# Weight sums of a Strassen-form projection taken from DRAM instead of formed by GpSimd

## The chip, the cores and the metric

The kernel runs on one core of a Trainium2 chip. The metric is the device time of one execution in microseconds (us). The engines are named TensorE (PE in the profile; PEld are its weight loads), VectorE (DVE), ScalarE (ACT), GpSimd (POOL) and SyncE (SP, which here only issues transfers).

## The reference

Two layers, each with two sub-layers on x of 512 tokens by 1024 features, all in float32:

```
for i in range(DEPTH):                                     # DEPTH = 2
    mix = mixer_sublayer(x, w_in[i], ...)                  # pooling mixer + bidirectional scan
    x = layer_norm(ALPHA * x + mix, ln1_g[i], ln1_b[i])
    ffn = conv_ffn(x, w_up[i], ffn_conv_w[i], ffn_conv_b[i], w_down[i])
    x = layer_norm(ALPHA * x + ffn, ln2_g[i], ln2_b[i])

def conv_ffn(x, w_up, ffn_conv_w, ffn_conv_b, w_down):
    h = dwconv_centred(x @ w_up, ffn_conv_w, ffn_conv_b)
    gate, val = jnp.split(h, 2, axis=-1)
    return (jax.nn.gelu(gate, approximate=False) * val) @ w_down
```

The scan of the mixer works on 32 heads, taken here in 8 units of 4 heads. w_down is 2816 by 1024. The change concerns the last product, with w_down, and the place in the mixer where the new transfers are issued.

## The kernel before, in words

Every float32 product is made of three TensorE passes on values split in a high part (wh, ah) and a remainder (wl, al). A weight block is loaded into a tile wraw (two places), ScalarE copies its rounded high part into wh (L90) and VectorE subtracts to get wl (L91); three places each for wh and wl. This is class WeightStream: a list of loads, and an order of cuts (`get`, `fill`) that runs ahead of TensorE. All loads go through SP's queue in the order of the list; a load waits there until its place is free.

A layer runs through the mixer, in which the eight units each make a decay matrix per head (m, fetched by ScalarE's queue as `m<-acd`, masked by GpSimd in L994, exponentiated by ScalarE in L1001), a state (xw by GpSimd in L1051, stp on TensorE, s in L1076) and an output y, begun by GpSimd in L1057 as `y = xtok * d_skip`; then through the up projection (TensorE into fg), and then the down stage (TensorE into dp_v, dp_x, dp_y, dp_z and a few more).

The down stage is in Strassen form (`strassen_projection`). The 22 k-tiles of w_down stand in 11 pairs, and each pair has four blocks of 128 by 512: b00, b01 (upper k-tile, left and right half) and b10, b11 (lower k-tile). Seven products take the place of eight, at the price of sums of blocks: t1 and t3 (L137, L138), t2 (L126) and t4 (L154) are formed by GpSimd in the kernel before, from blocks that lie in wraw. t1 and t3 replace their inputs in wraw; t2 goes into scratch (xths, xtls), and t4 replaces t2 there. The sums of the activations are made in the up stage; four of the seven are kept in SBUF, three (384 KB a pair) are spilled to DRAM (`asp<-r`, L1368) and fetched again in the down stage (`xtls<-asp`, L619, two places) and cut into dp_h and dp_l (L624, L625) one pair behind the fetch.

The loop over the first nine pairs, with the cuts `d` (b00 and b11) and `s` (t1 and t3), reads:

```
for i in range(n - 2):
    d, s = ws.get(), ws.get()
    both(vb, (tags[i], 3), d, 1, f, False)
    both(xb, ...); both(yb, ...); both(zb, ...)
    fetch(i)
    if i:
        cut(i - 1)
```

`both` makes two products of three passes each, so a pair takes 24 matmuls of 512 columns here and 18 in the lower phase (t2, b10, t4). A layer's down stage has 7 x 11 x 2 x 3 = 462.

TensorE's order is written out by hand. The orders of the other engines come from a scheduler, which places each instruction by priority and by when its inputs are ready.

Of the kernel before, what the change touches and what calls it, by code (L numbers as in the profile page):

```python
# [9 lines left out]
F32 = mybir.dt.float32  # L10
# [12 lines left out]
NL = 2  # L23
# [15 lines left out]
class WeightStream:  # L39
# [3 lines left out]
    def __init__(self, nc, tc, pool, plan, ahead, raw_bufs, bufs):  # L43
        self.nc, self.tc, self.pool = nc, tc, pool
        self.plan = plan
        self.subs = [(i, j) for i, r in enumerate(plan) for j in r["order"]]
        self.ahead = ahead
        self.raw_bufs, self.bufs = raw_bufs, bufs
        self.raw = {}
        self.done = {}  # L50
        self.next_raw = 0
        self.next_sub = 0
        self.pos = 0
        self.seq = []
        self.extra = {}
# [21 lines left out]
    def _split(self, s):  # L77
        i, view = self.seq[s]
        self.load(i + 1)
        src = view(self.raw[i])  # L80
        _, a, b = src.shape
        if s in self.extra:
            pool, bufs = self.extra[s]
        else:
            pool, bufs = self.pool, self.bufs
        h = pool.tile([P, 1024], F32R, tag="wh", name=f"wh{s}", bufs=bufs)
        l = pool.tile([P, 1024], F32R, tag="wl", name=f"wl{s}", bufs=bufs)
# [19 lines left out]
class StrassenWeights:  # L107
# [4 lines left out]
    def __init__(self, nc, tc, pairs):  # L112
        self.nc, self.tc, self.pairs = nc, tc, pairs
        self.t2 = {}
        self.raw0 = None

    def open(self, tiles):

        for t in tiles:
            for i in range(t.shape[1]):  # L120
                self.t2[len(self.t2)] = (t, i)
        self.make_t2(0, self.raw0)

    def make_t2(self, i, raw):
        t, j = self.t2[i]
        self.nc.gpsimd.tensor_tensor(  # L126
            t[:, j, :], raw[:, 1024:1536], raw[:, 512:1024], op=ALU.subtract
        )

    def direct(self, raw):  # L130

        return raw.rearrange("p (a b) -> p a b", a=2)[:, :, 0:512]

    def sums(self, i, raw):

        g = self.nc.gpsimd
        g.tensor_tensor(raw[:, 1536:2048], raw[:, 1024:1536], raw[:, 512:1024], op=ALU.subtract)  # L137
        g.tensor_tensor(raw[:, 512:1024], raw[:, 512:1024], raw[:, 0:512], op=ALU.subtract)  # L138
        if i:
            self.make_t2(i, raw)  # L140
        else:
            self.raw0 = raw
        return raw.rearrange("p (a b) -> p a b", a=2)[:, :, 512:1024]

    def two(self, q):
        t, j = self.t2[2 * q]
        return t[:, j : j + min(2, self.pairs - 2 * q), :]

    def lower(self, q, o, raw):

        t = self.two(q)
        n = t.shape[1]
        b = raw[:, o : o + n * 512].rearrange("p (a b) -> p a b", a=n)
        self.nc.gpsimd.tensor_tensor(t, b, t, op=ALU.subtract)  # L154
        return b

    def plan(self, w, first):

        raws, direct, sums = [], [], []
        for i in range(self.pairs):  # L160
            a, b = 2 * i * P, (2 * i + 1) * P
            raws.append({"srcs": [w[a : a + P, :].unsqueeze(1),
                                  w[b : b + P, 512:1024].unsqueeze(1)], "order": range(2)})
            direct.append((first + i, self.direct))
            sums.append((first + i, partial(self.sums, i)))
        seq = []
        for i in range(self.pairs - 2):
            seq += [direct[i], sums[i]]
        seq += direct[-2:] + sums[-2:]
        odd = w.rearrange("(k two p) c -> two p k c", two=2, p=P)[1, :, :, 0:512]  # L170
        lower, t2, t4 = [], [], []
        for i in range(0, self.pairs, 4):
            n = min(4, self.pairs - i)
            r = first + len(raws)
            raws.append({"srcs": [odd[:, i : i + n, :]], "order": range(n)})
            for k in range(0, n, 2):
                q = (i + k) // 2
                lower.append((r, partial(self.lower, q, k * 512)))
                t2.append((r if q else r - 1, lambda raw, q=q: self.two(q)))
                t4.append((r, lambda raw, q=q: self.two(q)))  # L180
# [44 lines left out]
def weight_plan(l, w_in, pool_w, w_ssd_proj, w_out, w_up, w_down, down):  # L225
# [71 lines left out]
    r, s = down.plan(w_down[l], len(raws))  # L297
# [4 lines left out]
def tile_hybrid_pool_ssd_convffn_encoder(  # L302
# [60 lines left out]
    downs = [StrassenWeights(nc, tc, KF // 2) for _ in range(NL)]  # L363
# [134 lines left out]
    class Norm:  # L498
# [28 lines left out]
        def add(self, c, c0, ps, first=False, last=False):  # L527
# [76 lines left out]
    def strassen_projection(l, name, sw, tags, pool, spill, norm):  # L604
# [7 lines left out]
        sw.open([scratch[0], scratch[1][:, : n - KD, :]])  # L612
        again = scratch[1][:, 3:6, :].rearrange("p a b -> p (a b)").rearrange(
            "p (s a b) -> p s a b", s=2, a=3)

        second = {}

        def fetch(i):
            nc.sync.dma_start(again[:, i % 2], spill[i])  # L619

        def cut(i):
            h = pool.tile([P, 4, 256], F32R, tag=f"ah{i}", name=f"{name}h{i}")
            lo = pool.tile([P, 4, 256], F32R, tag=f"al{i}", name=f"{name}l{i}")
            nc.scalar.copy(h[:, :3], again[:, i % 2])  # L624
            nc.vector.tensor_tensor(lo[:, :3], again[:, i % 2], h[:, :3], op=ALU.subtract)  # L625
# [20 lines left out]
        for i in range(n - 2):  # L646
# [12 lines left out]
            if i:  # L659
                cut(i - 1)  # L660
# [12 lines left out]
        for i in (n - 2, n - 1):  # L673
# [3 lines left out]
            cut(i - 1)  # L677
# [3 lines left out]
        for cc in range(2):  # L681
            norm.add(2 + cc, 512, zb[cc])
# [7 lines left out]
        for q in range(nq - 2):  # L690
# [5 lines left out]
            if q == 0:  # L696
                cut(n - 1)
# [70 lines left out]
    for l in range(NL):  # L768
# [264 lines left out]
        def unit_job(u, xtok, zs, xjobs):  # L1033
# [23 lines left out]
            nc.gpsimd.tensor_tensor(  # L1057
# [3 lines left out]
            )  # L1061
            ytiles[u] = (xtok, y)
# [278 lines left out]
        for j in range(KF):  # L1341
# [83 lines left out]
```

## Time and profile before

| | us |
|---|---|
| median of 3 runs | 1990.12 (1989.95 to 1991.82) |
| the profiled execution | 1992.83 |
| its span on the core | 1991.0 |
| TensorE busy | 1931.9 (97%) |
| VectorE busy | 1348.4 (68%) |
| ScalarE busy | 998.4 (50%) |
| GpSimd busy | 609.0 (31%) |

Layer 0's down stage runs from 872 to 993 us, layer 1's from 1857 to 1979. Matmuls overlap in the records: the distance from one start to the next is the time that one costs, not the length that its row gives.

### The profile page before, as it was taken

Reading aid. Unit: us, or ns where it says so; the run is one execution under the profiler, and the core shown is the slowest. Engines: PE = TensorE matmul, PEld = TensorE weight load, DVE = VectorE, ACT = ScalarE, POOL = GpSimd, SP = SyncE. Lnnn points to the kernel's source line nnn. Section 1 sums busy time; section 2 is a strip of 40 time slices with the busy share of each in tenths; the row PEclk is TensorE's granted clock in tenths of the full one; section 3 lists DMA queues with packets and bytes.
Section 4 is the critical chain, followed back from the end, with each engine's and each line's share of the span. In section 5 each row is a group of like instructions: output and inputs, shape, how many; then the busy total and the mean of one; then the engine's idle time right before and its main releaser. Section 6 shows DMA issues by size and latency. Waiting matters only on the chain.

```text
span 1991.0 us, 27368 instructions
## 1 busy us (share of the span) xinstructions
PE 1931.9 (97%) x10449; PEld 1616.0 (81%) x10449; DVE 1348.4 (68%) x1945; ACT 998.4 (50%) x1665; POOL 609.0 (31%) x578
## 2 busy tenths in 40 slices
PE   8999999999999999998999999999999999999997
PEld 7878798988888888876788878989888888888765
DVE  5668576775556656679985685667656566666898
ACT  4767666644333444444457776656443334444443
POOL 1244424241111111168303343242411111111773
PEclk9999999999999999999999999999999999999999
DMA  5444434233241334345225344343332414333541
GB/s 159 123 119 117 127 93 140 86 113 115 76 164 49 121 112 134 106 153 190 83 90 160 106 112 124 110 124 105 85 111 92 168 43 130 121 101 116 180 154 51
DMA packets 174691, 232.19 MB, mean 117 GB/s; under 512 B 7872, under 2 KB 128868, under 8 KB 174560
## 3 DMA queue, kind: packets, MB, share of 16 engines
q1 hardware_dynamic: 152144, 178.80, 28.3%
q10 hardware_dynamic: 17712, 34.08, 7.0%
q0 software_dynamic: 4704, 17.56, 2.5%
q8 instruction: 83, 1.36, 0.3%
q14 instruction: 48, 0.39, 0.1%
HBM read 217.31 MB, written 13.11 MB: 116 GB/s over the span
## 4 chain that ended last, share of the span: by engine, by line
PE 78%; DVE 6%; issue 6%; POOL 4%; DMA 3%; ACT 3%; SPq 0%; POOLq 0%; ACTq 0%; DVEq 0%
PE fg L382 7%; PE fg L381 7%; PE fg L383 7%; PE spp L381 3%; PE zp L381 3%; PE spp L382 3%; PE spp L383 3%; PE zp L382 3%; PE zp L383 3%; PE xp L381 3%; DVE wl L91 3%; PE xp L383 3%; PE xp L382 3%; PE stp L1068 2%; PE ydp L1019 2%
## 5 line engine op out<-in xcount | busy, mean ns | idle before, releaser
L91 DVE TENSOR_TENSOR wl<-wraw,wh 128x1024 fp32r<-128x1024 f32 (+1 forms) x330 | 454.1, 1377 | 251.6 <-ACT wh L90 250.0
L90 ACT CAST wh<-wraw 128x1024 fp32r<-128x1024 f32 (+1 forms) x330 | 341.2, 1035 | 503.6 <-PE fg L382 158.0
L383 PE MATMUL fg<-xthm,wl 128*128 128x512 f32 x640 | 249.0, 389 | 0.0
L381 PE MATMUL fg<-xthm,wh 128*128 128x512 f32 x640 | 249.0, 389 | 0.0
L382 PE MATMUL fg<-xtlm,wh 128*128 128x512 f32 x640 | 249.0, 389 | 0.0
L1001 ACT ACTIVATE m<-m,nac 128x128 f32<-128x128 f32 x512 | 159.6, 392 | 52.2 <-POOL m L994 51.7
L994 POOL TENSOR_SCALAR_AFFINE_SELECT m<-m 128x512 f32<-128x512 f32 x128 | 95.0, 765 | 183.5 <-DMA m<-acd 162.9
L381 PEld LDWEIGHTS fg<-xthm,wh 128*128 128x128 f32 x640 | 120.1, 188 | 25.0
L383 PEld LDWEIGHTS fg<-xthm,wl 128*128 128x128 f32 x640 | 120.1, 188 | 24.9
L382 PEld LDWEIGHTS fg<-xtlm,wh 128*128 128x128 f32 x640 | 120.1, 188 | 24.9
L1109 POOL TENSOR_TENSOR y<-y,yo 128x256 f32<-128x256 f32 x96 | 85.4, 898 | 101.6 <-DVE yo L1101 98.8
L381 PE MATMUL spp<-yth,wh 128*128 128x512 f32 x256 | 110.3, 431 | 0.5 <-ACT yth L1149 0.5
L382 PE MATMUL spp<-ytl,wh 128*128 128x512 f32 x256 | 101.2, 395 | 0.7 <-DVE ytl L1150 0.7
L383 PE MATMUL spp<-yth,wl 128*128 128x512 f32 x256 | 101.1, 395 | 0.0
L479 DVE SCALAR_TENSOR_TENSOR xc<-xp,pcwc,xc 128x510 f32<-128x510 f32 (+1 forms) x128 | 95.2, 745 | 7.2 <-ACT xc L473 5.7
L1002 DVE TENSOR_TENSOR m<-m 128x512 f32<-128x512 f32 x64 | 46.7, 730 | 64.8 <-ACT m L1001 55.5
L1051 POOL TENSOR_TENSOR xw<-xtok,wst 128x768 f32<-128x768 f32 x32 | 51.3, 1621 | 121.9 <-ACT xtok L943 99.0
L1363 POOL TENSOR_TENSOR r<-cvv,cg 128x512 f32<-128x512 f32 x22 | 28.4, 1292 | 175.1 <-issue 130.4
L381 PE MATMUL zp<-wh,xthf 128*128 128x256 f32 x256 | 77.6, 303 | 0.0
L1286 POOL TENSOR_TENSOR g<-g,acc 128x512 f32<-128x512 f32 x16 | 27.5, 1720 | 162.3 <-ACT g L1247 150.3
L381 PE MATMUL zp<-wh,xthi 128*128 128x256 f32 x256 | 77.1, 301 | 0.0
L382 PE MATMUL zp<-wl,xthf 128*128 128x256 f32 x256 | 73.0, 285 | 0.0
(403 smaller groups left out, 5214.0 us busy)
## 6 DMA issues: line engine op xcount, KB each, us to landing
wraw<-in_w_in_dram SPq DMA_DIRECT2D x56, 1024.0 KB, 5.5
wraw<-in_w_up_dram SPq DMA_DIRECT2D x44, 1024.0 KB, 5.2
m<-acd ACTq DMA_DIRECT2D x64, 512.0 KB, 4.9
wraw<-in_w_ssd_proj_dram SPq DMA_DIRECT2D x16, 1024.0 KB, 5.1
wraw<-in_w_down_dram SPq DMA_DIRECT2D x22, 512.0 KB, 3.6
asp<-r POOLq DMA_DIRECT2D x22, 384.0 KB, 2.9
xtls<-asp SPq DMA_DIRECT2D x22, 384.0 KB, 3.8
wraw<-in_w_in_dram SPq DMA_DIRECT2D x16, 512.0 KB, 5.3
```

Source lines behind the costliest of these rows:

```text
L90: self.nc.scalar.copy(hv, src)
L91: self.nc.vector.tensor_tensor(lv, src, hv, op=ALU.subtract)
L381: mm(lhsT=ah, rhs=bh, start=first, stop=False)
L382: mm(lhsT=ah, rhs=bl, start=False, stop=False)
L383: mm(lhsT=al, rhs=bh, start=False, stop=last)
L479: nc.vector.scalar_tensor_tensor(dst[:, o0:o1], ps[:, o0 + s : o1 + s], tap, dst[:, o0:o1], op0=ALU.mult, op1=ALU.add,)
L994: nc.gpsimd.affine_select(out=mv, in_=mv, pattern=[[0, NCH], [1 - 2 * d, P]], compare_op=ALU.is_ge, fill=NEG, base=0, channel_multiplier=2 ...
L1001: nc.scalar.activation(mc, mc, AF.Exp, bias=nac[:, c, col : col + 1])
L1002: nc.vector.tensor_tensor(m[:, 0], m[:, 0], m[:, 1], op=ALU.add)
L1019: nc.tensor.matmul(ps[q * 64 : (q + 1) * 64, c * 64 : (c + 1) * 64], lhsT=m[:, 0, t0 : t0 + 64], rhs=xtok[:, c, hh * 64 : (hh + 1) * 64], ...
L1051: nc.gpsimd.tensor_tensor(h4(xw[:, d]), h4(xtok[:, d : d + 3, :]), hb(wst, d, d + 3, d), op=ALU.mult)
L1109: nc.gpsimd.tensor_tensor(y[:, c, :], y[:, c, :], yo[:, d, :], op=ALU.add)
```

## The change

Three tensors in DRAM for each layer take the sums: t13 (t1 and t3 side by side), t2 and t4. They are filled by eight transfers from DRAM to DRAM on GpSimd's queue, of 1408 rows of 2 KB (2.88 MB) each. `prepare(u)` issues the u-th behind the instruction of L1057 of unit u: four plain copies in units 0 to 3, then four that add onto what is there, in units 4 to 7. The third of the adding ones reads t1 and the fourth reads t2, so each waits for an earlier transfer. The blocks are now added only; the signs that this turns are put right in the activations' sums and in the additions to the output, with as many instructions as before.

In the down stage GpSimd forms nothing. A pair's load is now b00, b11 (256 KB each) and t13's two blocks (512 KB); t2 and b10 come for two pairs at a time, t4 for four. The spilled sums get five places and are cut three pairs behind the fetch. The scratch that held t2 becomes two more places for loads (`raw_at`), and the first two cuts of t4 get places of their own (`cut_at`). The keys of `raw_at` count the loads of one layer, while the list of loads runs through both layers: in layer 0 two of four pairs go to the scratch, in layer 1 all loads go to wraw. The matmuls and their order are the same.

```diff
@@ WeightStream
+        self.raw_at = {}
+        self.cut_at = {}
...
-        raw = self.pool.tile([P, 2048], F32, tag="wraw", name=f"wraw{i}", bufs=self.raw_bufs)
+        if i in self.raw_at:
+            raw = self.raw_at[i]
+        else:
+            raw = self.pool.tile([P, 2048], F32, tag="wraw", name=f"wraw{i}",
+                                 bufs=self.raw_bufs)
...
+        if s in self.cut_at:
+            h, l = self.cut_at[s]
@@ StrassenWeights (open, make_t2, direct, sums, two, lower and the old plan are gone)
+    def __init__(self, nc, dram, l, w, pairs):
+        self.nc, self.pairs = nc, pairs
+        self.t13 = dram.tile([P, pairs, 2, 512], F32, name=f"t13_{l}")
+        self.t2 = dram.tile([P, pairs, 512], F32, name=f"t2_{l}")
+        self.t4 = dram.tile([P, pairs, 512], F32, name=f"t4_{l}")
+        self.blocks = w.rearrange("(k two p) (h c) -> two h p k c", two=2, h=2, p=P)
+        b, t1, t3 = self.blocks, self.t13[:, :, 0, :], self.t13[:, :, 1, :]
+        self.steps = [
+            (t1, b[0, 1]), (t3, b[0, 1]), (self.t2, b[1, 1]), (self.t4, b[1, 0]),
+            (t1, b[0, 0], ALU.add), (t3, b[1, 1], ALU.add),
+            (self.t2, t1, ALU.add), (self.t4, self.t2, ALU.add),
+        ]
+
+    def prepare(self, step):
+        dst, src, *op = self.steps[step]
+        if op:
+            self.nc.gpsimd.dma_start(dst, src, accum_op=op[0], max_dma_last_dim=2048)
         else:
+            self.nc.gpsimd.dma_start(dst, src)
+
+    def plan(self, first):
+        n, b = self.pairs, self.blocks
+        self.first = first
...
+        for i in range(n):
+            raws.append({"srcs": [b[0, 0, :, i : i + 1, :], b[1, 1, :, i : i + 1, :],
+                                  self.t13[:, i, :, :]], "order": range(2)})
+            direct.append((first + i, view(0)))
+            sums.append((first + i, view(1024)))
...
+        for i in range(0, n, 2):
+            m = min(2, n - i)
+            t2.append((first + len(raws), view(0, m)))
+            lower.append((first + len(raws), view(m * 512, m)))
+            raws.append({"srcs": [self.t2[:, i : i + m, :], b[1, 0, :, i : i + m, :]],
+                         "order": range(2)})
+        self.first_t4 = first + len(raws)
+        for i in range(0, n, 4):
...
+            raws.append({"srcs": [self.t4[:, i : i + m, :]], "order": range(2)})
@@ strassen_projection
-        sw.open([scratch[0], scratch[1][:, : n - KD, :]])
-        again = scratch[1][:, 3:6, :].rearrange("p a b -> p (a b)").rearrange(
-            "p (s a b) -> p s a b", s=2, a=3)
+        more = scratch[0].rearrange("p a b -> p (a b)").rearrange("p (s b) -> p s b", s=2)
+        for i in range(n):
+            if i % 4 > 1:
+                ws.raw_at[sw.first + i] = more[:, i % 2]
+        for i in range(2):
+            ws.raw_at[sw.first_t4 + i] = more[:, (n + i) % 2]
+        again = scratch[1].rearrange("p a b -> p (a b)")[:, : 5 * 768].rearrange(
+            "p (s a b) -> p s a b", s=5, a=3)
-        second = {}
+        second, lag = {}, 3
...
-            if i:
-                cut(i - 1)
+            if i >= lag:
+                cut(i - lag)
...
+        parts = base.tile([P, 4, 1024], F32R, tag="xtl", name=f"xtlp{l}")
+        for i in range(2):
+            ws.cut_at[ws.pos + 4 + i] = (parts[:, 2 * i], parts[:, 2 * i + 1])
...
-                norm.add(cc, 512, xb[cc])
-                norm.add(2 + cc, 512, xb[cc])
+                norm.add(cc, 512, xb[cc], op=ALU.subtract)
+                norm.add(2 + cc, 512, xb[cc], op=ALU.subtract)
@@ unit_job
-            nc.gpsimd.tensor_tensor(
+            skip = nc.gpsimd.tensor_tensor(
                 h4(y), h4(xtok),
...
+            with tc.issue_after(skip.ins):
+                downs[l].prepare(u)
@@ the activations' sums
-            nc.vector.tensor_tensor(q[:, 1], a21, r[:, 1], op=ALU.add)
+            nc.vector.tensor_tensor(q[:, 1], a21, r[:, 1], op=ALU.subtract)
...
-            nc.vector.tensor_tensor(q[:, 3], r[:, 0], r[:, 2], op=ALU.subtract)
+            nc.vector.tensor_tensor(q[:, 3], r[:, 0], r[:, 2], op=ALU.add)
```

GpSimd's order at unit 0 of layer 0 (y_0, xw_0 and s_0 are the unit's tiles, m_0 to m_2 its first heads' matrices), before and then after:

```order
L1057 TENSOR_TENSOR y_0_829<-xtok_0_424,dsk_158 128x1024
L994 AFFINE_SELECT m_0_775<-m_0_775 128x512 x2
L1051 TENSOR_TENSOR xw_0_826<-xtok_0_424,wst_752 128x768
L994 AFFINE_SELECT m_1_792<-m_1_792 128x512 x2
L1051 TENSOR_TENSOR xw_0_826<-xtok_0_424,wst_752 128x768
L1076 TENSOR_TENSOR s_0_2_921<-s_0_1_902,tot_763 128x512
L994 AFFINE_SELECT m_2_809<-m_2_809 128x512 x2
```

```order
L1058 TENSOR_TENSOR y_0_835<-xtok_0_430,dsk_164 128x1024
L995 AFFINE_SELECT m_0_781<-m_0_781 128x512 x2
L140 DMA t_0_83<-in_w_down_dram 1408x1x512
L995 AFFINE_SELECT m_1_798<-m_1_798 128x512 x2
L1052 TENSOR_TENSOR xw_0_832<-xtok_0_430,wst_758 128x768 x2
L995 AFFINE_SELECT m_2_815<-m_2_815 128x512 x2
L1079 TENSOR_TENSOR s_0_2_928<-s_0_1_909,tot_769 128x512
```

The transfer into t13 (t_0_83) stands behind the first two m, and both xw, which stood apart, now stand together behind four m.

GpSimd's order at unit 7 of layer 0, before and then after (t_0_84 is t2, t_0_85 is t4):

```order
L1057 TENSOR_TENSOR y_7_4284<-xtok_7_3791,dsk_158 128x1024
L785 DMA dsk_8534<-in_d_skip_dram 128x32
L994 AFFINE_SELECT m_31_4323<-m_31_4323 128x512 x2
L1076 TENSOR_TENSOR s_7_2_4398<-s_7_1_4364,tot_763 128x512
L1076 TENSOR_TENSOR s_7_3_4438<-s_7_2_4398,tot_763 128x512
```

```order
L1058 TENSOR_TENSOR y_7_4297<-xtok_7_3803,dsk_164 128x1024
L138 DMA t_0_85<-t_0_84 1408x512
L995 AFFINE_SELECT m_31_4337<-m_31_4337 128x512 x2
L1079 TENSOR_TENSOR s_7_2_4412<-s_7_1_4378,tot_769 128x512
L786 DMA dsk_8528<-in_d_skip_dram 128x32
L1079 TENSOR_TENSOR s_7_3_4452<-s_7_2_4412,tot_769 128x512
```

The adding transfer into t4 stands directly behind y_7 and ahead of m_31 and the states.

SP's order at the start of layer 0's down stage (wraw and xths are places for loads, asp the spilled sums), before and then after:

```order
L66 DMA wraw_7556<-in_w_down_dram 128x1024
L66 DMA wraw_7556<-in_w_down_dram 128x512
L66 DMA wraw_7666<-in_w_down_dram 128x1024
L66 DMA wraw_7666<-in_w_down_dram 128x512
L619 DMA xtls_7655<-asp_91 128x768
L66 DMA wraw_7705<-in_w_down_dram 128x1024
L66 DMA wraw_7705<-in_w_down_dram 128x512
```

```order
L72 DMA wraw_7570<-in_w_down_dram 128x512 x2
L72 DMA wraw_7570<-t_0_83 128x1024
L72 DMA wraw_7678<-in_w_down_dram 128x512 x2
L72 DMA wraw_7678<-t_0_83 128x1024
L72 DMA wraw_7787<-in_w_down_dram 128x512 x2
L72 DMA wraw_7787<-t_0_83 128x1024
L617 DMA xtls_7668<-asp_97 128x768
L72 DMA xths_7667<-in_w_down_dram 128x512 x4
L72 DMA xths_7667<-t_0_83 128x1024 x2
```

The loads of pairs 0, 1 and 4 go to wraw, those of pairs 2 and 3 to xths; the latter now stand behind pair 4's load and the first fetch.

SP's order at the start of layer 1's down stage, after (t_1_86 is t13 of layer 1):

```order
L72 DMA wraw_15919<-in_w_down_dram 128x512 x2
L72 DMA wraw_15919<-t_1_86 128x1024
L72 DMA wraw_16027<-in_w_down_dram 128x512 x2
L72 DMA wraw_16027<-t_1_86 128x1024
L72 DMA wraw_16064<-in_w_down_dram 128x512 x2
L72 DMA wraw_16064<-t_1_86 128x1024
L617 DMA xtls_16017<-asp_98 128x768 x5
L72 DMA wraw_16101<-in_w_down_dram 128x512 x2
L72 DMA wraw_16101<-t_1_86 128x1024
```

Every load goes to wraw, three ahead of the fetches, and then one fetch follows each load.

## Rows read from the trace of the kernel before

**Rows 1.** The page, its first line and busy time by engine.
```profile
span 1991.0 us, 27368 instructions
...
PE 1931.9 (97%) x10449; PEld 1616.0 (81%) x10449; DVE 1348.4 (68%) x1945; ACT 998.4 (50%) x1665; POOL 609.0 (31%) x578
```

**Rows 2.** Windows: stretch, length, busy us (instructions) of each engine, clock, DMA.
```profile
660.00:760.00 100.00, 100.00 (x443) 82.81 (x442) 62.98 (x81) 43.07 (x52) 15.47 (x20) 1.00 0.37 121
871.70:990.00 118.30, 109.85 (x455) 85.45 (x454) 108.46 (x97) 51.72 (x58) 77.39 (x42) 0.99 0.47 148
1857.00:1983.00 126.00, 111.93 (x498) 87.61 (x496) 116.49 (x122) 53.19 (x61) 79.40 (x41) 1.00 0.41 134
890.00:900.00 10.00, 8.26 (x35) 6.11 (x34) 9.94 (x5) 5.57 (x6) 9.11 (x6) 1.00 0.83 291
```

**Rows 3.** Waits of TensorE, whole run: us in total, times, longest.
```profile
PE dp_v L382 <- DVE wl L91: 14.3, 18, 1.8
...
PE stp L1068 <- POOL xw L1051: 6.3, 4, 2.0
...
PE dp_y L382 <- DVE epsdp__7651 L509: 1.4, 1, 1.4
...
PE ydp L1019 <- ACT m L1001: 1.0, 2, 0.6
```

**Rows 4.** Timeline of VectorE, layer 0's entry and layer 1's loop: start, length.
```profile
878.89 1.22 DVE L91 TENSOR_TENSOR wl<-wraw,wh 128x1024 fp32r<-128x1024 f32 x1
880.02 0.95 DVE L625 TENSOR_TENSOR dp_l<-xtls,dp_h 128x768 fp32r<-128x768 f32 x1
...
1881.40 4.55 DVE L91 TENSOR_TENSOR wl<-wraw,wh 128x1024 fp32r<-128x1024 f32 x2
1885.88 2.05 DVE L625 TENSOR_TENSOR dp_l<-xtls,dp_h 128x768 fp32r<-128x768 f32 x1
1887.84 4.55 DVE L91 TENSOR_TENSOR wl<-wraw,wh 128x1024 fp32r<-128x1024 f32 x2
```

**Rows 5.** Timeline of GpSimd in layer 1's loop.
```profile
1884.83 2.27 POOL L137 TENSOR_TENSOR wraw<-wraw 128x512 f32<-128x512 f32 x1
1887.18 1.89 POOL L138 TENSOR_TENSOR wraw<-wraw 128x512 f32<-128x512 f32 x1
1889.15 2.16 POOL L126 TENSOR_TENSOR xths<-wraw 128x512 f32<-128x512 f32 x1
```

**Rows 6.** Lines of GpSimd: count, busy us, mean ns, idle before by releaser.
```profile
L154 POOL TENSOR_TENSOR xths<-wraw,xths 128x1024 f32<-128x1024 f32 x8 | 21.9, 2738 | 33.0 <-DVE wl L91 20.3 <-DMA wraw<-in_w_down_dram 12.7
```

**Rows 7.** The same view, a transfer issued from GpSimd.
```profile
L1368 POOL DMA_DIRECT2D asp<-r x22 | 12.9, 584 | 31.3 <-DVE q L1367 26.9 <-issue 4.4
```

**Rows 8.** Timeline of GpSimd, layer 0's mixer, units 1, 6 and 7.
```profile
124.76 1.89 POOL L1057 TENSOR_TENSOR y<-xtok,dsk 128x1024 f32<-128x1024 f32 x1
...
133.88 1.04 POOL L1076 TENSOR_TENSOR s<-s,tot 128x512 f32<-128x512 f32 x1 [5.06 <-DVE s L1083]
...
385.09 1.89 POOL L1057 TENSOR_TENSOR y<-xtok,dsk 128x1024 f32<-128x1024 f32 x1
...
426.19 1.90 POOL L1057 TENSOR_TENSOR y<-xtok,dsk 128x1024 f32<-128x1024 f32 x1 [1.34 <-DVE zs L1114]
```

**Rows 9.** The page, one DMA queue and the issues: KB each, us to landing.
```profile
q0 software_dynamic: 4704, 17.56, 2.5%
...
wraw<-in_w_in_dram SPq DMA_DIRECT2D x56, 1024.0 KB, 5.5
...
m<-acd ACTq DMA_DIRECT2D x64, 512.0 KB, 4.9
...
wraw<-in_w_down_dram SPq DMA_DIRECT2D x22, 512.0 KB, 3.6
...
wraw<-in_w_down_dram SPq DMA_DIRECT2D x22, 256.0 KB, 3.9
```

**Rows 10.** The tile m, its transfers.
```profile
DMA to landing us min/median/max: 4.5/4.9/7.9
```

More of the change, by code (lines that the diff above doesn't have):

```diff
@@ L81, in _split @@
         _, a, b = src.shape
-        if s in self.extra:
-            pool, bufs = self.extra[s]
-        else:
-            pool, bufs = self.pool, self.bufs
-        h = pool.tile([P, 1024], F32R, tag="wh", name=f"wh{s}", bufs=bufs)
-        l = pool.tile([P, 1024], F32R, tag="wl", name=f"wl{s}", bufs=bufs)
+        if s in self.cut_at:
+            h, l = self.cut_at[s]
+        else:
+            pool, bufs = self.extra.get(s, (self.pool, self.bufs))
+            h = pool.tile([P, 1024], F32R, tag="wh", name=f"wh{s}", bufs=bufs)
+            l = pool.tile([P, 1024], F32R, tag="wl", name=f"wl{s}", bufs=bufs)
         hv = h[:, : a * b].rearrange("p (a b) -> p a b", a=a)
@@ L107 @@
 class StrassenWeights:
[L112 to L128, printed above, removed]
@@ L145, in two @@
[L145 to L157, printed above, removed]
-        raws, direct, sums = [], [], []
[L160 to L165, printed above, removed]
+    def __init__(self, nc, dram, l, w, pairs):
[10 more added lines that the diff above has]
+        ]
@@ L166, in plan @@
         seq = []
-        for i in range(self.pairs - 2):
+        for i in range(n - 2):
             seq += [direct[i], sums[i]]
         seq += direct[-2:] + sums[-2:]
-        odd = w.rearrange("(k two p) c -> two p k c", two=2, p=P)[1, :, :, 0:512]
         lower, t2, t4 = [], [], []
[L172 to L180, printed above, removed]
@@ L181, in plan @@
-        nq = len(t2)
-        for q in range(nq - 2):
+        for i in range(0, n, 2):
[6 more added lines that the diff above has]
+        for i in range(0, n, 4):
+            m = min(4, n - i)
+            for k in range(0, m, 2):
+                t4.append((first + len(raws), view(k * 512, min(2, m - k))))
+            raws.append({"srcs": [self.t4[:, i : i + m, :]], "order": range(2)})
@@ L183, in plan @@
+        for q in range(len(t2) - 2):
             seq += [t2[q], lower[q]]
@@ L296, in weight_plan @@
         seq += [a[0], b[0], a[1], b[1]]
-    r, s = down.plan(w_down[l], len(raws))
+    r, s = down.plan(len(raws))
     return raws + r, seq + s
@@ L362, in tile_hybrid_pool_ssd_convffn_encoder @@
     raws, seq = [], []
-    downs = [StrassenWeights(nc, tc, KF // 2) for _ in range(NL)]
+    downs = [
+        StrassenWeights(nc, dram, l, w_down[l], KF // 2) for l in range(NL)
+    ]
     for l in range(NL):
@@ L525, in root, with add @@
             return y
-        def add(self, c, c0, ps, first=False, last=False):
+        def add(self, c, c0, ps, first=False, last=False, op=ALU.add):
             c1 = c0 + ps.shape[1]
@@ L623, in cut @@
             lo = pool.tile([P, 4, 256], F32R, tag=f"al{i}", name=f"{name}l{i}")
-            nc.scalar.copy(h[:, :3], again[:, i % 2])
-            nc.vector.tensor_tensor(lo[:, :3], again[:, i % 2], h[:, :3], op=ALU.subtract)
+            nc.scalar.copy(h[:, :3], again[:, i % 5])
+            nc.vector.tensor_tensor(lo[:, :3], again[:, i % 5], h[:, :3], op=ALU.subtract)
             second[i] = (h, lo)
@@ L676, in strassen_projection @@
             fetch(i)
-            cut(i - 1)
+            cut(i - lag)
         for cc in range(2):
@@ L695, in strassen_projection @@
                 both(vb, (second[k], 0), b21, k - 2 * q, k == 0, False)
-            if q == 0:
-                cut(n - 1)
+            if q < lag:
+                cut(n - lag + q)
+        parts = base.tile([P, 4, 1024], F32R, tag="xtl", name=f"xtlp{l}")
+        for i in range(2):
+            ws.cut_at[ws.pos + 4 + i] = (parts[:, 2 * i], parts[:, 2 * i + 1])
         t2 = [ws.get(), ws.get()]
```

20 lines of the change are left out of this document (6 added, 14 removed).

## Prediction

> **What bounds the kernel now.** I read the page's totals first: TensorE is busy 97% of the span, GpSimd 31% [rows 1]. So the kernel is bound by TensorE almost everywhere, and an edit pays only where TensorE is held up. The windows say where. In 100 us of the up projection 443 matmuls fill the whole stretch, 100/443 = 0.226 us each. In the 118.3 us of layer 0's down stage there are 455 matmuls of the same 512 columns, 0.260 us each, with TensorE idle for 118.30 - 109.85 = 8.45 us; GpSimd and VectorE, lightly loaded in the first stretch, are busy for 77 and 108 us of the second [rows 2]. The waits name the cause: the longest sum on TensorE in the whole run is dp_v for VectorE's wl, 14.3 us in 18 waits [rows 3], so nine in each layer, one for each turn of the loop over pairs.
>
> VectorE is late because its instructions stretch. Beside no GpSimd work a wl takes 1.22 us and a dp_l 0.95 us; in the loop two wl take 4.55 us and a dp_l 2.05 us, and the two together come round every 1887.84 - 1881.40 = 6.44 us [rows 4]. GpSimd's three sums of one pair fill the same round: 2.27 + 1.89 + 2.16 = 6.32 us [rows 5]. TensorE needs 24 matmuls for a pair, 24 x 0.226 = 5.42 us. So the loop is set by GpSimd and VectorE, which slow each other, and TensorE waits 1.0 us in every pair. The lower blocks are no better: L154 waits for VectorE and for loads ahead of its 2.74 us instructions [rows 6].
>
> **Removed.** All GpSimd sums of the down stage: 77.4 + 79.4 us of GpSimd's work, nearly all that these windows hold [rows 2]. Without them VectorE needs 2 x 1.22 + 0.95 = 3.39 us a pair against TensorE's 5.42, so TensorE sets the stage. The gain of a layer is bounded from layer 0's row: at least the idle 8.45 us, at most 118.3 - 455 x 0.226 = 15.5 us, since the matmuls beside the waits are spaced wider too. Nine turns of 1.02 us make 9.2 us before the lower blocks are counted, which fits between. I take the middle, 12.0 us, less the 1.4 us that dp_y waits for eps in each layer [rows 3], which nothing here removes: 10.6 us, and 21.2 us for both layers.
>
> **Added to GpSimd's queue.** Eight transfers a layer, each issued behind y of its unit and ahead of that unit's m, s and xw. The nearest row is a GpSimd transfer of 128 rows, 584 ns to issue [rows 7]. These have 1408 rows: between 0.58 us, if the count doesn't matter, and 11 x 0.58 = 6.4 us, if it is all that matters. Behind y of the second unit GpSimd idles 5.06 us after an s and two m [rows 8], so an issue below about 5 us lies in idle time, except in the first units, where TensorE already waits for xw (6.3 us in four waits) [rows 3]: there an issue, and xw moved behind two m, counts in full. I take the value near the row, 0.6 us for each of two units and a little for the moved xw: 1 us a layer, 2 us in all. At 6.4 us it would be (6.4 - 5) x 16 = 22 us, the whole gain; at best nothing.
>
> The last two transfers also wait: t2 for t1's accumulation two units before, t4 for t2's, one unit before. Behind the waiting instruction stand m and s, and ScalarE and TensorE behind those. Between the two y of these units lie 426.19 - 385.09 = 41.1 us [rows 8]. The GpSimd queue moved 17.56 MB in 2.5% of the 16 engines' 1991 us, so at 353 GB/s [rows 9]; 2.88 MB (1408 rows of 2 KB) take 8.2 us so, an accumulation that reads twice perhaps 16 us, and with half the engines 33 us. All are under 41 us, so no wait.
>
> **Added to the DMA engines.** Sixteen such transfers run beside the mixer's loads. An m lands in 4.5 to 7.9 us, median 4.9 [rows 10], and TensorE waited for m only 1.0 us in the run [rows 3]: the slowest landing, 3 us late, cost nearly nothing. So the cost is nothing at one end; at the other each transfer makes one m late by another 4.9 us, of which 3 are covered: 16 x 1.9 = 30 us. The weight loads take 5.5 us [rows 9] for weights cut well ahead. I take 0, by the row of waits, and keep the 30 for the range.
>
> The Trainium skill, in "DMA: Bandwidth & Descriptors", section "Issuing engines are not separate DMA queues", speaks against the change: transfers run on the same 16 engines and interleave, whoever issued them. The landings cited bear on this but do not test it: the longest of them, 7.9 us, is not tied to another queue there. By the rule alone the sum would move from 0 toward the 30 us above.
>
> **The stage's loads.** A pair now needs 1024 KB of weights and 384 KB of spilled sums in 5.42 us, 266 GB/s; the busiest 10 us of the stage before moved 291 GB/s [rows 2]. In layer 1 the loads have only wraw's two places. A place is held for two cuts, about two turns of half a pair (5.4 us), and may take 2 x 5.42 - 5.4 = 5.4 us to fill; before, 512 KB landed in 3.6 us and 256 KB in 3.9 beside each other [rows 9]. If a cut comes at once upon landing, the hold shrinks to ScalarE's and VectorE's work, some 3.5 us, and 7.3 us remain: enough, barely. In layer 0 the scratch gives two more places, but pair 2's load stands on SP behind pair 4's, which waits for pair 0's place. Three loads of 1024 KB at 291 GB/s are 10.8 us from there; pair 2 is wanted about two pairs, 10.8 us, after the start. Between 0 and 4 us, and I take 1. The added plus and minus signs change no instruction count.
>
> **The sum.** 21.2 - 2 - 0 - 1 = 18 us. The profiled execution took 1992.83 us around its span of 1991.0; 1975 after. The median shown lies 2.7 us under it, so 1972.
>
> **Rivals.**
> *GpSimd is held while its transfers drain.* If an issue lasts as long as the transfer, 8.2 us for a copy and 16.4 for an accumulation, the 5 us of idle behind y cover part: 4 x (3.2 + 11.4) = 58 us a layer, 117 in both, less the 21: about 2085. If the idle of 5 us comes twice in a unit, 4 x (0 + 6.4) x 2 = 51 less 21: about 2020. It decides at a hold of 5 + 18/16 = 6.1 us. For it: these have eleven times the rows of any GpSimd transfer seen. Against it: 584 ns for 384 KB that land in 2.9 us [rows 7, 9], so issue and transfer are apart at that size.
> The Trainium skill, "Perfetto Trace Analysis", section "DMA Instruction — SWDGE (GPSIMD)", says that GpSimd's time on a transfer ends with its last descriptor, and that engines may begin earlier when there are more descriptors than the buffer holds. That would tie the issue to the transfer here; no run before shows a buffer filling.
> *The transfers crowd m.* The 30 us end above: 1972 + 30 = 2002, or about 1990 with half of it, no change.
> *Layer 1's two places set the round.* If a load takes 8.5 us, the round is (8.5 + 3.5)/2 = 6.0 us and layer 1 keeps 0.44 of 1.02 us a pair: 6 us lost, 1978. At 9.4 us the round is 6.44, nothing is won in layer 1, and the time is 1983.
> *The stage was really bound by loads.* Then the added 256 KB a pair give it back, about 1990. Against it: wl, not a load, is what TensorE waits for.
>
> **How the numbers follow.** Forecast, all steps as above: 0.55, range 1961 (15.5 us a layer kept, nothing paid) to 1977. Two places set the round: 0.18, 1977 to 1985. GpSimd held: 0.12. Crowded m, slower: 0.07; crowded or load-bound and unchanged: 0.08. A difference under 0.2%, 4 us, can't be told from none here. Faster: 0.55 + 0.18 = 0.73; unchanged 0.08; slower 0.19. The range reaches from 1958, with some of L154's waits gone beyond the layer's bound, to 2000.
>
> **What would show it.** In the down stage of the changed profile no TensorE wait for wl, wl near 1.22 us, dp_l near 0.95 us, and 455 matmuls in about 106 us. The 16 transfers of GpSimd well under 5 us to issue, y to s no longer than before, and TensorE's waits for xw and m within 1 or 2 us of before. Wrong would be: issues of 8 us or more; m landing in 10 us with TensorE waiting on m; a wl that waits for a load in layer 1; or a wl still at 2.2 us with GpSimd idle, which would put VectorE's stretch down to something else.

## The result and the profile after

The changed kernel takes 2057.82 us (median of 4 runs, 2055.51 to 2060.37) against 1990.97 us for the kernel before on the same chips: 1.0333 times as long, 95% interval 1.0315 to 1.0351. The forecast was 1972 us, the range 1958 to 2000. The span of its profiled execution is 2058.6 us.

Where the 67.6 us of span went is read from the start of the first matmul of each stage (fu of the up projection, dp_v of the down stage, dbc of the next layer's mixer):

| stage, us | before | after |
|---|---|---|
| layer 0 to its first fu (mixer, output projection) | 625.1 | 672.7 |
| layer 0, up projection | 246.8 | 246.8 |
| layer 0, down stage, to layer 1's first dbc | 123.0 | 112.1 |
| layer 1 to its first fu | 615.7 | 658.4 |
| layer 1, up projection | 246.8 | 246.8 |
| layer 1, down stage and end | 133.6 | 121.8 |

The down stages won 10.9 + 11.8 = 22.7 us. The mixers lost 47.6 + 42.7 = 90.3 us.

First the part that came as forecast. The windows of the two down stages after, with the columns of [rows 2]:

```profile
919.30:1030.50 111.20, 109.23 (x475) 88.09 (x474) 81.67 (x110) 53.45 (x62) 7.39 (x9) 1.00 0.70 240
1936.60:2047.50 110.90, 108.39 (x497) 88.64 (x495) 80.94 (x106) 52.15 (x58) 6.10 (x6) 1.00 0.63 219
```

TensorE idles 2.0 and 2.5 us in a stage where it idled 8.45 [rows 2], and GpSimd and VectorE have fallen from 77 and 108 us of work to about 7 and 81. The timeline of VectorE in layer 1's loop shows why, beside [rows 4]:

```profile
1957.16 2.52 DVE L97 TENSOR_TENSOR wl<-wraw,wh 128x1024 fp32r<-128x1024 f32 x2 [1.85 <-ACT wh L96]
1959.92 0.96 DVE L623 TENSOR_TENSOR dp_l<-xtls,dp_h 128x768 fp32r<-128x768 f32 x1 [0.24 <-ACT dp_h L622]
```

Two wl in 2.52 us instead of 4.55, a dp_l in 0.96 instead of 2.05, and VectorE now waits between them.

Now the mixers. The waits of TensorE over the whole run, beside [rows 3]:

```profile
PE ydp L1020 <- DVE m L1013: 34.0, 7, 8.8
PE yop L1098 <- DVE yo L1104: 11.8, 2, 7.0
PE xt L810 <- ACT xc L804: 6.3, 2, 3.2
PE zp L374 <- ACT wh L96: 5.4, 2, 2.7
...
PE stp L1071 <- POOL xw L1052: 1.1, 2, 0.7
```

dp_v is gone from the list. ydp, the product that reads m, has taken its place with seven waits of up to 8.8 us. The transfers of the changed kernel, from the list of issues (KB each, median us to landing), beside [rows 9]:

```profile
t<-in_w_down_dram POOLq DMA_DIRECT2D x12, 2816.0 KB, 17.7
m<-acd ACTq DMA_DIRECT2D x64, 512.0 KB, 7.4
...
t<-t POOLq DMA_DIRECT2D x4, 2816.0 KB, 26.3
```

m lands after 7.4 us in the middle where it took 4.9. Its slowest landing, from the view of the tile m, beside [rows 10]:

```profile
DMA to landing us min/median/max: 4.6/7.4/14.3
```

GpSimd is the first to use m. Its group of that line, from the costliest groups of the page (busy us, mean ns | idle before it, and what ended most of that), first before, then after:

```profile
L994 POOL TENSOR_SCALAR_AFFINE_SELECT m<-m 128x512 f32<-128x512 f32 x128 | 95.0, 765 | 183.5 <-DMA m<-acd 162.9
```

```profile
L995 POOL TENSOR_SCALAR_AFFINE_SELECT m<-m 128x512 f32<-128x512 f32 x128 | 92.6, 750 | 297.8 <-DMA m<-acd 279.2
```

GpSimd already stood 162.9 us for m's landing before, and stands 116.3 us more now.

The longest of TensorE's waits can be followed from engine to engine. The timeline at unit 1 of layer 0 (start, length; compare unit 1 in [rows 8]):

```profile
125.46 1.01 POOL L140 DMA_DIRECT2D t<-in_w_down_dram  x1
...
130.68 0.37 ACTq L990 DMA_DIRECT2D m<-acd  x1
...
131.11 0.48 ACTq L990 DMA_DIRECT2D m<-acd  x1
...
134.62 1.05 POOL L1079 TENSOR_TENSOR s<-s,tot 128x512 f32<-128x512 f32 x1 [8.15 <-ACT s L1077]
...
142.54 1.22 POOL L995 TENSOR_SCALAR_AFFINE_SELECT m<-m 128x512 f32<-128x512 f32 x2 [6.87 <-DMA m<-acd]
...
148.72 1.12 PE L1020 MATMUL ydp<-xtok,m 128*64 128x64 f32 x16 [8.81 <-DVE m L1013]
```

The transfer goes out at 125.46. Two loads of m go out 5 us later, and land 11.7 and 12.6 us after that. GpSimd stands 6.87 us for the first, ScalarE and VectorE behind it, and TensorE 8.81 us at the end. The chain of waits names the same link in the same place:

```profile
130.68 11.74 DMA m<-acd
142.55 0.13 POOL m L995
...
147.93 0.70 DVE m L1013
148.72 1.12 PE ydp L1020 x16
```

The loss is more than the waits. The windows before, in and after this one:

```profile
130.00:140.00 10.00, 9.91 (x75) 8.62 (x73) 3.54 (x5) 5.45 (x10) 1.05 (x1) 1.00 0.99 246
140.00:149.00 9.00, 0.28 (x5) 0.31 (x7) 3.27 (x4) 6.50 (x17) 4.39 (x5) 0.67 0.65 202
149.50:153.50 4.00, 4.00 (x16) 3.14 (x14) 1.02 (x2) 1.89 (x3) 1.22 (x2) 0.53 0.31 67
154.50:158.00 3.50, 3.50 (x23) 3.06 (x22) 1.23 (x1) 2.07 (x4) 0.00 (x0) 1.00 0.73 126
```

While the transfer ran, the DMA engines were busy 99% of the time. TensorE then idled, and its granted clock was 0.53 in the 4 us behind the wait, near the lower of its two levels (1.2 and 2.4 GHz). Matmuls of 512 columns started 0.43 us apart there, and 0.23 us apart after it (start, length):

```profile
150.80 0.63 PE L376 MATMUL xp<-xthi,wl 128*128 128x512 f32 x1
151.23 0.63 PE L374 MATMUL xp<-xthi,wh 128*128 128x512 f32 x1
...
153.57 0.40 PE L374 MATMUL xp<-xthi,wh 128*128 128x512 f32 x1
153.80 0.39 PE L375 MATMUL xp<-xtli,wh 128*128 128x512 f32 x1
```

### The profile page after: what moved, and what is told of

Same layout as the page of the kernel before. It is cut to its first block, busy times and chain, and to the rows that moved or that the text cites. A ratio compares the mean times of both kernels' runs of the same rounds, so it can differ in the third digit from the quotient of the medians.

```text
span 2058.6 us, 27344 instructions
## 1 busy us (share of the span) xinstructions
PE 1951.0 (95%) x10449; PEld 1635.0 (79%) x10449; DVE 1292.9 (63%) x1945; ACT 998.4 (48%) x1667; POOL 464.7 (23%) x516
## 4 chain that ended last, share of the span: by engine, by line
PE 61%; DMA 13%; issue 12%; DVE 5%; ACT 5%; POOL 4%; SPq 0%; ACTq 0%; POOLq 0%; DVEq 0%
DMA m<-acd 9%; PE fg L376 7%; PE fg L374 7%; PE fg L375 7%; DMA wraw<-in_w_in_dram 3%; ACT m L1002 2%; PE g0p L374 1%; PE spp L374 1%; PE spp L375 1%; PE spp L376 1%; PE g1p L375 1%; PE g1p L374 1%; PE g0p L375 1%; PE g0p L376 1%; DVE wl L97 1%
## 5 line engine op out<-in xcount | busy, mean ns | idle before, releaser
L97 DVE TENSOR_TENSOR wl<-wraw,wh 128x1024 fp32r<-128x1024 f32 (+1 forms) x338 | 422.4, 1251 | 334.0 <-ACT wh L96 328.1
L96 ACT CAST wh<-wraw 128x1024 fp32r<-128x1024 f32 (+1 forms) x338 | 346.3, 1027 | 465.4 <-PE fg L375 161.9
L1002 ACT ACTIVATE m<-m,nac 128x128 f32<-128x128 f32 x512 | 159.7, 390 | 82.1 <-POOL m L995 80.3
L556 POOL TENSOR_TENSOR x<-x,lnb 128x512 f32<-128x512 f32 x15 | 21.1, 1408 | 292.7 <-DVE x L552 286.5
L1020 PEld LDWEIGHTS ydp<-xtok,m 128*64 128x64 f32 x1024 | 37.9, 146 | 53.4 <-issue 46.4
L1020 PE MATMUL ydp<-xtok,m 128*64 128x64 f32 x1024 | 46.9, 238 | 34.0 <-DVE m L1013 34.0
L375 PE MATMUL zp<-wl,xthi 128*128 128x256 f32 x256 | 74.2, 290 | 2.8 <-DVE wl L97 2.8
## 6 DMA issues: line engine op xcount, KB each, us to landing
t<-in_w_down_dram POOLq DMA_DIRECT2D x12, 2816.0 KB, 17.7
t<-t POOLq DMA_DIRECT2D x4, 2816.0 KB, 26.3
```

Of the source, the lines that this page charges most:

```text
L375: mm(lhsT=ah, rhs=bl, start=False, stop=False)
L556: (nc.vector if last else nc.gpsimd).tensor_tensor(x1, x1, bt[:, 512:], op=ALU.add)
L1002: nc.scalar.activation(mc, mc, AF.Exp, bias=nac[:, c, col : col + 1])
L1020: nc.tensor.matmul(ps[q * 64 : (q + 1) * 64, c * 64 : (c + 1) * 64], lhsT=m[:, 0, t0 : t0 + 64], rhs=xtok[:, c, hh * 64 : (hh + 1) * 64], ...
```

## The experiments

Two theories of the loss were to be told apart. Theory 1: the transfers share the DMA engines with loads that TensorE needs soon, above all m. Theory 2: the scheduler, which counts on the transfers, gave the mixer another order, and the order costs the time. GpSimd's own time on the transfers is a third cause, and a rival of the forecast.

**No transfers.**

```diff
-            with tc.issue_after(skip.ins):
-                downs[l].prepare(u)
...
-                                  self.t13[:, i, :, :]], "order": range(2)})
+                                  self.w[2 * i * P : (2 * i + 1) * P, :].unsqueeze(1)], "order": range(2)})
```

> The changed kernel without its sixteen transfers: the down stage loads the same bytes straight from w_down, so the sums of weight blocks are left out of the result. Theory 1 (the transfers share the DMA engines with m, m lands late, TensorE waits in the mixer) and theory 2 (the order that the scheduler gave the mixer because of the transfers) both expect the whole 90 us lost in the mixers back and the 21 us won in the down stages kept: about 1968 us. The mixer's order here is that of the kernel before, so this run alone does not tell 1 from 2. If the time stays above 2000 us, the loss lies in something else that the change brought, such as the loads of the down stage.

1967.27 us, 0.9877 of the kernel before (0.986 to 0.9893). The mixer stages are back at 624.4 and 615.5 us, the down stages at 110.4 and 121.2. So the whole loss hangs on the transfers, and the gain in the down stages, 25 us of span, is real.

**The transfers in the up projection.**

```diff
-                downs[l].prepare(u)
...
+            kept = nc.gpsimd.dma_start(asp[l][i], r)
+            if i in (0, 1, 2, 3, 4, 5, 7, 9):
+                with tc.issue_after(kept.ins):
+                    downs[l].prepare({7: 6, 9: 7}.get(i, i))
```

> The changed kernel with the same sixteen transfers issued in the up projection, behind the spill of pairs 0 to 5, 7 and 9. Theory 1 expects the mixers' 90 us back, because no m is loaded there, and a small or no cost in the up projection, whose weights are loaded a whole tile ahead: 1968 to 1975 us. A theory that the bytes cost whatever they run beside (each transfer takes 17 to 30 us of the DMA engines from any load) expects TensorE to wait for w_up's cuts instead: 2010 us or more.

1979.68 us, 0.9938 (0.9922 to 0.9954): faster than before, and between the two expectations. The mixer stages are 626.8 and 615.2 us, the up projections 246.8 and 245.3, unharmed by the same bytes at DMA shares of 0.62 to 0.97. The time lost against the kernel without transfers (12 us between the medians, 16.3 between the profiled spans) stands nearly all in the down stages, 120.3 and 127.1 us, 9.9 and 5.9 more than there. Their two waits for a first cut, from TensorE's waits (6.2 us is layer 0's):

```profile
PE dp_v L374 <- ACT wh L96: 7.1, 2, 6.2
```

Layer 0's last transfer, issued at 862 us and landed 25.7 us later, ran into the loads with which the stage begins at 874.

**The same traffic beside the kernel before.**

```diff
+    extra = [Transfers(nc, dram, l, w_down[l], KF // 2) for l in range(NL)]
...
+            with tc.issue_after(skip.ins):
+                extra[l].prepare(u)
```

> The kernel before with the same sixteen transfers behind the same y, into tensors that nothing reads; its down stage is unchanged. Theory 1 and theory 2 expect the full loss of the mixers, 90 us, without the gain: about 2081 us. If the loss needed the other parts of the change as well, the time stays under 2040 us.

2072.71 us, 1.0408 (1.0393 to 1.0424). The mixer stages are 663.1 and 658.0 us, 80.3 us above before, the down stages as before (124.6 and 132.5). So the transfers make a loss with the old down stage as with the new one, but 80 us of it and not the full 90: layer 0's mixer loses 38.0 us here and 47.6 in the changed kernel. Why is not shown.

**The transfers in pieces.**

```diff
+                with tc.issue_after(cut.ins):
+                    downs[l].prepare(h // 4, h % 4)
...
+        a, z = 3 * part, min(3 * part + 3, self.pairs)
+        dst, src = dst[:, a:z], src[:, a:z]
```

> The changed kernel with each transfer cut in four pieces of at most three pairs (0.79 MB), one behind the mask of each head, so that the mixer carries the same bytes in 64 pieces. If what costs is the length of the burst that an m meets (theory 1: 17 us of a rival transfer, m 7 us late), a piece of 0.79 MB delays an m by 3 us at most, which the rows of before showed to be covered: 1970 to 1995 us. If what costs is the bytes, or the share of the engines (a form of theory 1 with no slack at all), or GpSimd's time on issues (64 issues of some 0.6 us or more), the time stays near 2050 us.

2032.72 us, 1.0205 (1.0189 to 1.022): both expectations missed. The mixers lose 34.1 + 30.5 = 64.6 us against the kernel without transfers, where the whole transfers lose 48.3 + 42.9 = 91.2. From its list of issues:

```profile
m<-acd ACTq DMA_DIRECT2D x64, 512.0 KB, 6.6
t<-in_w_down_dram POOLq DMA_DIRECT2D x36, 768.0 KB, 7.5
...
t<-t POOLq DMA_DIRECT2D x12, 768.0 KB, 11.3
```

A piece lands in less than half the time of a whole transfer, and m after 6.6 us instead of 7.4. TensorE's longest waits in it:

```profile
PE zp L376 <- ACT wh L96: 15.9, 4, 7.3
PE stp L1073 <- POOL xw L1056: 9.8, 9, 3.3
```

No wait of ydp for m is left among the longest; waits for weights (wh) and for xw stand there. A wait for wh can still go back to m. Before layer 0's longest one, of 6.4 us, which ends at 380.88 us, the timeline of ScalarE has:

```profile
364.61 0.37 ACTq L992 DMA_DIRECT2D m<-acd  x1
...
375.48 1.28 ACT L1004 ACT_TABLE_LOAD   x1 [5.66 <-DMA m<-acd]
...
379.79 1.03 ACT L96 CAST wh<-wraw 128x1024 fp32r<-128x1024 f32 x1
```

ScalarE stood 5.66 us for an m that landed 10.8 us after its issue, and cut wh behind it. The load of these weights was late too: it landed at 376.3 us, 14.8 us after its issue. So shorter bursts help m, and the same bytes still make loads of m and of weights late.

**Retimed in the up projection.**

```diff
+            if i < 8:
+                with tc.issue_after(kept.ins):
+                    downs[l].prepare((0, 1, 4, 5, 2, 6, 3, 7)[i])
```

> The sixteen transfers in the up projection, one behind the spill of each of pairs 0 to 7, in the order t1, t3, add to t1, add to t3, t2, add to t2, t4, add to t4, so that the last one is issued some 41 us before the down stage instead of 16. In the first try the last addition ran into the down stage's first loads and TensorE waited 6.2 us for a cut there in layer 0. Theory 1 (a transfer costs only where a load with little slack runs beside it) expects that wait gone: 1967 to 1972 us, the time without transfers. If the up projection's own loads pay, or if the transfers slow later loads in another way, it stays at 1978 to 1982 us.

1970.28 us, 0.9896 (0.988 to 0.9912), as theory 1 had it. The down stage of layer 0 takes 111.4 us again. The five runs spread from 1966.61 to 1977.15 us, and the slowest is the profiled one. In it the up projection of layer 1 takes 252.0 us where the others take 246.8 at most, behind one wait of TensorE for a cut of w_up:

```profile
PE fg L374 <- ACT wh L96: 3.2, 1, 3.2
```

So the up projection can pay too; how often it does is not shown.

**Four places for loads in both layers.**

```diff
-        self.first = first
+        self.first = first + self.base
...
+        downs[l].base = len(raws)
```

> As the kernel before it in this list, with the places of loads in the scratch keyed by the position in the whole list, so that layer 1 has four places for loads as layer 0 has. If two places held layer 1 back, 2 to 6 us less; if, as the profile of the changed kernel shows (its layer 1 down stage takes 110.1 us from the first to the last matmul, layer 0's 110.5), two are enough, no difference above 2 us.

1966.22 us, 0.9874 (0.986 to 0.9889). That is 4 us below the kernel above it, but the runs of the two overlap (1963.38 to 1969.23 and 1966.61 to 1977.15), so a gain from the places is not shown. It is the fastest complete kernel of this study, 1.3% below the kernel before, and it stands within 1.1 us of the one without any transfers: in these four runs the sixteen transfers in the up projection cost nothing that can be measured. Its two down stages:

```profile
872.30:984.00 111.70, 109.74 (x475) 87.66 (x473) 83.31 (x113) 54.27 (x63) 7.41 (x9) 1.00 0.71 245
1844.80:1954.50 109.70, 108.48 (x496) 88.30 (x494) 80.95 (x111) 51.52 (x58) 5.84 (x6) 1.00 0.64 224
```

**Copies in place of additions.**

```diff
-            self.nc.gpsimd.dma_start(dst, src, accum_op=op[0], max_dma_last_dim=2048)
+            self.nc.gpsimd.dma_start(dst, src)
```

> The changed kernel with the eight accumulating transfers replaced by plain copies of the same shape at the same place (the additions are left out of the result). An accumulation lands in 21 to 31 us, a copy in 15 to 19. If the loss goes with the time for which a transfer is in flight, 8 copies of 17 us stand for 4 x 17 + 4 x 27, that is 77% of the loss: about 1967 + 0.77 x 90 = 2037 us. If it goes by the number of transfers, 2057 us. If the accumulation itself (GpSimd's 1.75 us issue, waiting for an earlier transfer) were the cost, 2015 us or less.

2037.03 us, 1.0226 (1.0211 to 1.0242), the number of the first expectation. The next but one shows that the rule behind it does not hold.

**Small transfers.**

```diff
+            self.nc.gpsimd.dma_start(dst[:, :1], src[:, :1], accum_op=op[0], max_dma_last_dim=2048)
...
+            self.nc.gpsimd.dma_start(dst[:, :1], src[:, :1])
```

> The changed kernel with transfers of one pair (128 rows) in place of eleven, at the same place behind y; the down stage loads straight from w_down, so the sums are left out of the result. GpSimd issues as many transfers and waits for earlier ones in the same way. Theory 1 (bytes in flight beside m and the weights) expects 1967 to 1971 us, the time without transfers. If GpSimd's issues, or what stands behind them on GpSimd, cost the time, 1990 us or more. The mixer's order is here that of the kernel before, so a time near 1967 leaves open a part of the loss that comes from the order.

1968.56 us, 0.9886 (0.9872 to 0.9899). As many issues on GpSimd, each tied to the same earlier transfers, an eleventh of the bytes, and no loss. An issue takes 0.53 to 0.88 us here, so it is the rows below that have to show what the full ones take from GpSimd. The issues of the full transfers in the changed kernel, beside [rows 7], from the lines of GpSimd:

```profile
L140 POOL DMA_DIRECT2D t<-in_w_down_dram x8 | 8.2, 1020 | 0.0
L138 POOL DMA_DIRECT2D t<-in_w_down_dram x4 | 7.0, 1756 | 0.0
L138 POOL DMA_DIRECT2D t<-t x4 | 6.1, 1516 | 0.0
```

1.0 us for a copy and 1.5 to 1.8 for an addition, 21.3 us in both layers together and no idle time before them, while the transfers land after 17.7 and 26.3 us (medians): GpSimd was not held, and its time on the transfers is too short to be the 90 us.

**Half of the transfers.**

```diff
+            if u < 4:
+                with tc.issue_after(skip.ins):
+                    downs[l].prepare(u)
...
+            if i in (0, 2, 4, 6):
+                with tc.issue_after(kept.ins):
+                    downs[l].prepare(4 + i // 2)
```

> The four copies of a layer stay in the mixer's units 0 to 3, the four additions go to the up projection (behind the spills of pairs 0, 2, 4 and 6). If the loss goes with the time in flight, 4 x 17 of 4 x 17 + 4 x 27 us remain, 39% of 90: about 2002 us. If each transfer costs the same, 50%: 2012 us. If only the additions, or only the first units, made the loss, 1970 or 2050 us.

2019.74 us, 1.0144 (1.0127 to 1.016): outside every expectation. The mixers lose 28.4 + 26.4 = 54.8 us with four copies each, so 6.9 us for a copy in units 0 to 3. With copies only, all eight lost 37.6 + 35.6 = 73.2, so a copy in units 4 to 7 cost (73.2 - 54.8)/8 = 2.3 us; with additions there (91.2 - 54.8)/8 = 4.5 us. These prices take the parts of the loss as a plain sum, which no run tests. By them the loss does not go with the time in flight alone; the place counts more.

Which place, the matmuls tell, for TensorE's order in the mixer is the same in all these kernels. Compare the starts of the same matmul in layer 0, with the time that it has in the kernel without transfers. The changed kernel lags by nothing at 130 us, behind unit 0's transfer; by 30.6 at 230, behind those of units 1 and 2; by 32.8 at 350, behind those of units 3 and 4; by 48.3 at 430, behind those of units 5 and 6; and by no more to the end of the mixer. With half of the transfers the lag is 28.4 us at 230 and stays so. So units 1 and 2 make nearly all of the four copies' loss in layer 0, and four of the eight transfers there cost next to nothing.

**m made short.**

```diff
+                w = T if h < 3 else T // 8
+                    m[:, :, :w],
...
+                if w < T:
+                    nc.gpsimd.memset(m[:, :, w:], NEG)
```

> The changed kernel with m's transfers cut to an eighth (64 KB instead of 512 KB, the rest of m is filled by GpSimd, so the decay matrices are left out of the result); the sixteen transfers and their places stay. Theory 1 in its narrow form (m, which has three places and lands late, is what the transfers cost) expects the short m to land in 3 to 6 us beside a transfer and most of the 90 us back: 1970 to 1990 us. If the late weights of the mixer carry the loss, or both, 2010 to 2055 us.

2023.9 us, 1.0168 (1.0144 to 1.0192). The mixers still lose 27.2 + 25.4 = 52.6 us. The run does not test what it was meant to, because the short m lands late too. (GpSimd's filling of m also gave the mixer a third order.) m's transfers in the windows 88 to 124 us, with none of the sixteen transfers in flight, and 405 to 430 us, behind an addition issued at 406.57:

```profile
L991 ACTq DMA_DIRECT2D m<-acd x4: 366/367/367, 90.7 to 109.6; - x4
DMA to landing us min/median/max: 2.9/2.9/4.0
...
L991 ACTq DMA_DIRECT2D m<-acd x4: 366/366/367, 407.5 to 426.7; - x4
DMA to landing us min/median/max: 6.4/9.3/11.3
```

64 KB land after 2.9 us (one of the four after 4.0) without a transfer and after 6.4 to 11.3 us beside the addition. Over the run, 25 of the 39 short loads that met a transfer took 6.4 us or more. So an m is not late because of its own bytes. TensorE's longest wait is the same as in the changed kernel:

```profile
PE ydp L1024 <- DVE m L1017: 31.2, 6, 6.6
```

What is shown: the bytes of the transfers in the mixer make the loss (none, small, up and before plus), m is late beside them, and TensorE waits behind it. Theory 2 is not needed for most of the loss. In the kernels without transfers in the mixer, with small ones, or with transfers in the up projection the scheduler's order of the mixer was that of the kernel before, and with full transfers, as additions or copies, it was the changed one; with half of the transfers it lay between the two. There order and traffic moved together. The kernel with the transfers in pieces parts them: of the 226 instructions of GpSimd and the 647 of VectorE in layer 0's mixer, 2 and 25 stand elsewhere than in the kernel without transfers, where the changed kernel has 52 and 100. It has nearly the order of before and all of the bytes, and its mixers lose 64.6 us of the 91.2. What stays open are the other 26.6 us, which may be the order's or the longer bursts', and in the 64.6 the share of GpSimd's time on 64 issues (63 us in all). How the loss divides between m and the weights is not settled either.

## Why the prediction was wrong

**What failed: the term "added to the DMA engines".** The prediction took 0 for it, with 30 us as its other end. The mixers lost 90.3 us, 5.6 for each of the sixteen transfers; 80.3 with the old down stage and 64.6 with the transfers in pieces and nearly the old order. Three of its parts were off.

The reading of "the slowest landing, 3 us late, cost nearly nothing". TensorE's 1.0 us of waits for m [rows 3] was taken as room of 3 us behind every m. But the one late landing may have met a place with room. The row that GpSimd stood 162.9 us for m's landing before was not read: in those places no landed m lies ready in front of GpSimd, and a late m can pass its lateness on to ScalarE, VectorE and TensorE, as it does at 142 us in the timeline above.

The count: "each transfer makes one m late". The transfers were taken for 8.2 and perhaps 16 us long; they landed after 17.7 and 26.3 (medians), and met one to four loads of m each, 40 in all.

The size: "by another 4.9 us", as if two loads shared the engines evenly. Of the 40 loads of m that met a transfer 24 landed 10 to 14 us after their issue, 5 to 9 late; the others took 4.7 to 8.7 us. The short m shows that an even share of bytes is the wrong picture: an eighth of the bytes landed after 6.4 to 11.3 us.

Behind the waits comes the lower clock, which the prediction left out of this term: the window at 149.5 us has 0.53.

The Trainium skill's rule in "DMA: Bandwidth & Descriptors", section "Issuing engines are not separate DMA queues", was cited against the change and given no weight in the sum. The trace agrees with it: 24 loads of m on ScalarE's queue landed 5 to 9 us late beside transfers from GpSimd's.

**The rivals.** "The transfers crowd m" came nearest, at a chance of 0.07 for slower and priced a third of what it took; late weights, which it does not name, have a share. "GpSimd is held while its transfers drain" would have given 2020 to 2085 us and so the measured time, for the wrong reason: issues took 1.0 to 1.8 us, within the forecast bounds of 0.58 and 6.4. "Layer 1's two places set the round" did not happen: its down stage lost 2.5 us idle, and four places showed no gain outside the spread.

**What held.** The down stages: 21.2 us less 1 for layer 0's entry were forecast, 22.7 measured (the kernel without transfers has 25.0). wl and dp_l fell to 1.26 and 0.96 us, as the cause named (GpSimd and VectorE slowing each other) demands, and dp_v's 18 waits for wl were gone (two waits for later cuts of VectorE's were left, 0.8 and 1.1 us). One part of that sum was wrong, a small one: the two waits of 1.4 us for eps, which it kept, were gone as well. The waits of t2 and t4 for earlier additions cost nothing: those additions landed after 27 to 31 us, and 41 lie between the two y. The added bytes of the stage were carried: 240 and 219 GB/s.

**The chances.** Faster had 0.73. All of them rested on a mixer that was judged by TensorE's waits alone. Windows of 50 us in layer 0's mixer before, where the transfers of units 0, 1 and 5 went:

```profile
50.00:100.00 50.00, 50.00 (x356) 43.75 (x355) 29.65 (x49) 37.45 (x69) 15.23 (x16) 1.00 0.50 125
100.00:150.00 50.00, 46.45 (x314) 39.67 (x314) 31.59 (x42) 33.31 (x71) 20.18 (x22) 0.97 0.45 118
...
350.00:400.00 50.00, 50.00 (x369) 45.49 (x368) 37.90 (x66) 29.74 (x59) 12.93 (x13) 1.00 0.28 86
```

Around unit 1 TensorE already idled for 3.55 us in 50, and there the loss is largest. But the DMA share does not rank the places: unit 0's transfer, at the highest share of the three, cost nothing that lasted, and unit 5's cost about 6 us at the lowest, where TensorE was full. These rows would have warned, not given the price.

## What to carry to other kernels

A transfer in the background is not free because its own result is wanted late: look at which loads run beside it, how many places they have, and whether the engine that takes them already waits for their landing; move the transfer to a stage whose loads run far ahead, and let it end before the next stage begins. An engine that waits for a landing and is waited for in turn shows in its own waits, not in those of the engine at the end. And before a price is put on a shared resource, count how many of the short loads a long one spans.

## What the runs showed of the hardware

Loads of 64 KB that took 2.9 to 4.0 us without a transfer took 6.4 to 11.3 us in a stretch beside one transfer of 2.88 MB from another queue, where loads of 512 KB (4.9 us in the median before) mostly took 10 to 14 us.

A transfer of 1408 rows of 2 KB from DRAM to DRAM landed after 14.6 to 19.0 us as a copy in the changed kernel, and after 21.1 to 30.9 us as an addition. GpSimd's issue took 1.0 us for the copy and 1.5 to 1.8 us for the addition, against 0.53 to 0.58 and 0.82 to 0.88 us for 128 rows (the small transfers), so it grew about twofold for eleven times the rows.

A wait of 8.8 us costs TensorE more than 8.8 us: in the 4 us behind it the granted clock was 0.53 and matmuls of 512 columns started 0.43 us apart instead of 0.23.
